# RWKV-7 chunk products written in turn to both column halves, on one Trainium2 core

## The chip, the cores and the metric

The kernel is one program on one core of a Trainium2 chip. The metric is the device time of one launch in microseconds (us), lower is better. The core has engines that run side by side, each in the order in which its instructions were written down: PE (TensorE, matrix products out of SBUF into PSUM; its weight loads are listed as PEld), DVE (VectorE) and ACT (ScalarE), which can both read PSUM, POOL (GpSimd), and SP (SyncE), which issues most DMAs. An engine waits where its next instruction needs something that another has not done yet, and everything behind that instruction waits with it.

## The reference

One layer of a hybrid block over T = 2064 tokens (16 learned ones and 2048 of input) with width 1024: a combined input projection, three head groups beside each other (an RG-LRU recurrence, attention with a forgetting gate, RWKV-7), an output projection with a norm, and a gated feed-forward part with a short convolution. The change touches only the RWKV-7 group, which has 4 heads of 64. For each head it runs this recurrence over a 64x64 state S:

```python
def step(S, inp):
    r_t, w_t, k_t, v_t, kk_t, a_t = inp
    s_kk = jnp.einsum('bhij,bhj->bhi', S, kk_t)
    S = S * w_t[:, :, None, :] - s_kk[..., None] * (kk_t * a_t)[:, :, None, :] + v_t[..., None] * k_t[:, :, None, :]
    return S, jnp.einsum('bhij,bhj->bhi', S, r_t)
_, o = lax.scan(step, s0, xs)
mean = jnp.mean(o, axis=-1, keepdims=True)
var = jnp.mean(jnp.square(o - mean), axis=-1, keepdims=True)
o = ((o - mean) * lax.rsqrt(var + GN_EPS)).reshape(bsz, t, RWKV_WIDTH) * ln_w + ln_b
```

## The kernel before, in words

**Stages.** The input projection runs in three parts over tokens (tiles psp; lines L168 to L170 are the three products of a split fp32 product). Beside it a second stream of work is threaded in, `recurrences`: the gates, the RG-LRU blocks and the RWKV blocks. Attention follows (scores sc at L659 and L660, maxima mx at L530, values po at L682), then the output projection, the feed-forward part up and down. The RWKV work is longer than the projection: its blocks 5 to 8 run beside attention.

**An RWKV block** (`Rwkv.block`, `Rwkv.chunks`) is 4 chunks of 64 tokens, the ninth and last block one chunk. An item is a chunk of one head; a block has ni = 16 items (m2 = 8 chunk pairs of two heads: p is the pair of heads, h the head in it). `sc` holds an item's score matrices, `w3` its transposed operands. The recurrence within a chunk becomes a triangular solve (16x16 blocks on POOL and DVE, joined into 32 and then 64 wide by the small products L1158 into `xf`). The products behind the solve are the ones that change:

- L1198: 16 products a block, 64 rows by 64 columns with 64 moving columns, eight in one PSUM tile, all into partitions 0 to 63. ACT copies each tile into `w3` (L1201).
- L1207: 16 products with 128 moving columns, four in a tile, partitions 0 to 63. DVE copies the left half of each into `ap` (tile xu, L1208), ACT the right half into `w3` (L1209).
- L1222: 16 products like L1207's in size, but head h writes to partitions 64h to 64h+63, so that neighbours take turns. DVE adds the tile to `gt` and `rp` (L1223 and the next line).
- L1234 and L1242, the states: one PSUM tile `gain` holds the gain of all four chunks (L1234, 128 rows), and then chunk after chunk the old state is multiplied in (L1242, four products a chunk) and DVE copies the new state out to `st` (L1246), which the next chunk needs.
- L1274 and L1279, the outputs: for head 0 and then for head 1 a PSUM tile is filled by `rp` times state (L1274) and by scores times values (L1279); the chunks take turns between the two partition halves. Then come the mean and variance over a head on DVE.

**PSUM.** All of these tiles (`self.ps()`, rps in the profile) come from one tag with two buffers: a third tile waits until the first has been copied out.

**What sets the order.** The program's text gives each engine's instructions and their dependencies, and the framework's scheduler, which runs over a simulated timeline, sets the order in which they stand on each engine, RWKV's products among those of the projection and of attention. So an edit of one product moves others too. In the rows of the order below, the names are tiles with buffer numbers (out<-operands), and x8 means eight products in a row.

Of the kernel before, what the change touches and what calls it, by code (L numbers as in the profile page):

```python
# [12 lines left out]
AF = mybir.ActivationFunctionType  # L13
# [5 lines left out]
P = 128  # L19
# [924 lines left out]
class Rwkv:  # L944
# [127 lines left out]
    def chunks(self, b, nch, sg, rav, bk, wc, bon):  # L1072
# [120 lines left out]
        yield  # L1193
        for i0 in range(0, ni, 8):
            m = min(8, ni - i0)
            ps = self.ps().rearrange("p (i t) -> p i t", t=64)
            for i in range(m):
                nc.tensor.matmul(  # L1198
                    ps[0:64, i], sc[64:128, i0 + i, 128:192], w3[64:128, i0 + i, 0:64], start=True, stop=True
                )  # L1200
            nc.scalar.activation(w3[0:64, i0 : i0 + m, 64:128], ps[0:64, :m], AF.Copy)  # L1201
        ap = self.t([P, 2, ni, 64], "xu")[0:64, 0]
        for i0 in range(0, ni, 4):
            m = min(4, ni - i0)
            ps = self.ps().rearrange("p (i t) -> p i t", t=P)
            for i in range(m):
                nc.tensor.matmul(ps[0:64, i], xf[:, i0 + i], w3[0:64, i0 + i], start=True, stop=True)  # L1207
            nc.vector.tensor_copy(ap[:, i0 : i0 + m], ps[0:64, :m, 0:64])  # L1208
            nc.scalar.activation(w3[0:64, i0 : i0 + m, 0:64], ps[0:64, :m, 64:128], AF.Copy)  # L1209
        yield  # L1210
# [19 lines left out]
        for c in range(nch):  # L1230
            for h in range(2):
                for p in range(2):
                    j = 2 * (p * nch + c) + h
                    nc.tensor.matmul(  # L1234
                        gain[64 * h : 64 * h + 64, c, p], sc[:, j, 0:64], w3[:, j, 0:64],
                        start=c == 0 and p == 0, stop=False, skip_group_check=True,
                    )
        for c in range(nch):
            for h in range(2):
                hs = slice(64 * h, 64 * h + 64)  # L1240
                for p in range(2):
                    nc.tensor.matmul(  # L1242
                        gain[hs, c, p], gt[hs, p * nch + c], st[hs, c, p], start=False, stop=True,
                        skip_group_check=True,
                    )
            nc.vector.tensor_copy(st[:, c + 1], gain[:, c])  # L1246
# [14 lines left out]
        v4 = lambda t: t.rearrange("p q a h t -> p (q a) h t")  # L1261
        for h in range(2):
            hs = slice(64 * h, 64 * h + 64)
            ps = self.ps()[:, : P * ntl].rearrange("p (q a t) -> p q a t", a=2, t=64)

            for kind in range(2):
                for p in range(2):
                    for c in range(nch):
                        q, u = divmod(c, 2)
                        pc = p * nch + c  # L1270
                        j = 2 * pc + h
                        dst = ps[64 * u : 64 * u + 64, q, p]
                        if kind == 0:
                            nc.tensor.matmul(  # L1274
                                dst, rp[hs, pc], st[hs, c, p], start=p == 0 and q == 0, stop=False,
                                skip_group_check=True,
                            )
                        else:
                            nc.tensor.matmul(  # L1279
                                dst, sc[:, j, 64:128], w3[:, j, 0:64], start=False, stop=True, skip_group_check=True  # L1280
                            )
            mh = mean[:, :, h : h + 1]
# [877 lines left out]
```

## Time and profile before

| what | us |
|---|---|
| median of 3 runs | 3096.74 |
| lowest and highest of them | 3089.53, 3121.2 |
| the profiled execution | 3106.4 |
| its span | 3104.7 |
| PE busy in the 335 us from 865 | 296.53 |
| PE busy with RWKV's products before 865 and after | 139.64, 110.44 |
| busy in L1198, L1207 | 21.41, 37.78 |
| busy in L1222, L1234 | 18.57, 10.30 |
| busy in L1242, L1274, L1279 | 17.72, 19.60, 12.72 |

The profile is of one execution. An engine's busy time is the time in which at least one of its instructions ran; matmuls overlap, so a line's mean times its count is more than its busy time. In the timeline rows a stretch is a run of like instructions on one engine. The granted clock is the share of TensorE's full clock that the throttle let through.

### The profile page before, as it was taken

Reading aid. Unit: us, or ns where it says so; the run is one execution under the profiler, and the core shown is the slowest. Engines: PE = TensorE matmul, PEld = TensorE weight load, DVE = VectorE, ACT = ScalarE, POOL = GpSimd, SP = SyncE. Lnnn points to the kernel's source line nnn. Section 1 sums busy time; section 2 is a strip of 40 time slices with the busy share of each in tenths; the row PEclk is TensorE's granted clock in tenths of the full one; section 3 lists DMA queues with packets and bytes.
Section 4 is the critical chain, followed back from the end, with each engine's and each line's share of the span. In section 5 each row is a group of like instructions: output and inputs, shape, how many; then the busy total and the mean of one; then the engine's idle time right before and its main releaser. Section 6 shows DMA issues by size and latency. Waiting matters only on the chain.

```text
span 3104.7 us, 52180 instructions
## 1 busy us (share of the span) xinstructions
PE 2923.7 (94%) x18488; PEld 2496.3 (80%) x18488; DVE 2167.8 (70%) x4231; ACT 1462.1 (47%) x2770; POOL 1302.0 (42%) x1436
## 2 busy tenths in 40 slices
PE   6998999999979998899989899999999999999998
PEld 6987988998856664565558899999999999787776
DVE  6247655676688678677635889897778777547766
ACT  4145434344534444445544555566666665324333
POOL 3310101100124465445743568743533334556765
PEclk8999999999968789999999999999999999999999
DMA  6664333353353235543336555565665565535444
GB/s 210 223 203 141 105 96 100 106 142 106 94 128 90 67 84 132 127 114 102 87 99 200 158 181 168 169 197 168 164 168 162 168 187 160 180 101 173 149 161 143
DMA packets 455478, 443.71 MB, mean 143 GB/s; under 512 B 81472, under 2 KB 372490, under 8 KB 452384
## 3 DMA queue, kind: packets, MB, share of 16 engines
q1 hardware_dynamic: 454832, 439.98, 48.3%
q8 instruction: 145, 2.38, 0.3%
q14 instruction: 117, 0.96, 0.1%
q0 software_dynamic: 384, 0.39, 0.0%
HBM read 314.39 MB, written 125.87 MB: 142 GB/s over the span
## 4 chain that ended last, share of the span: by engine, by line
PE 63%; DVE 12%; DMA 11%; POOL 6%; issue 4%; ACT 3%; SPq 1%; POOLq 0%; DVEq 0%; ACTq 0%
PE psu L168 7%; PE psu L169 7%; PE psu L170 7%; PE psp L169 4%; PE psp L170 4%; PE psp L168 4%; PE po L682 3%; PE psd L169 2%; PE psd L168 2%; PE psd L170 2%; PE pswo L168 2%; PE pswo L170 2%; PE pswo L169 2%; DVE uw L1569 2%; PE mx L530 2%
## 5 line engine op out<-in xcount | busy, mean ns | idle before, releaser
L168 PE MATMUL psu<-xo,uw 128*128 128x344 f32 x1848 | 592.7, 325 | 23.3 <-DVE vb L1724 11.7
L169 PE MATMUL psu<-xo,uw 128*128 128x344 f32 x1848 | 594.2, 322 | 0.0
L170 PE MATMUL psu<-xo,uw 128*128 128x344 f32 x1848 | 583.9, 321 | 0.0
L170 PE MATMUL psp<-xh,wl 128*128 128x384 f32 (+2 forms) x1152 | 378.3, 329 | 3.2 <-DVE wl L163 3.2
L168 PE MATMUL psp<-xh,wh 128*128 128x384 f32 (+2 forms) x1152 | 380.5, 330 | 0.0
L169 PE MATMUL psp<-xl,wh 128*128 128x384 f32 (+2 forms) x1152 | 378.3, 328 | 0.0
L168 PEld LDWEIGHTS psu<-xo,uw 128*128 128x128 f32 x1848 | 348.2, 189 | 30.3 <-DVE vb L1724 15.1
L1569 DVE TENSOR_TENSOR uw<-uq,uw 128x512 fp32r<-128x512 f32 x352 | 333.9, 955 | 53.2 <-ACT uw L1568 49.6
L169 PEld LDWEIGHTS psu<-xo,uw 128*128 128x128 f32 x1848 | 349.5, 189 | 0.3 <-DVE xo L1569 0.3
L170 PEld LDWEIGHTS psu<-xo,uw 128*128 128x128 f32 x1848 | 347.8, 189 | 0.0
L1568 ACT ACTIVATE uw<-uq 128x512 fp32r<-128x512 f32 x462 | 286.4, 627 | 89.0 <-PE psu L170 38.4
L664 ACT ACTIVATE p<-sc,bias 128x512 f32<-128x512 f32 (+4 forms) x352 | 197.2, 591 | 189.8 <-PE sc L660 165.1
L1680 DVE SCALAR_TENSOR_TENSOR uy<-psu,ffn_cols,uy 128x342 f32<-128x342 f32 (+1 forms) x396 | 223.6, 566 | 70.6 <-ACT uy L1678 69.6
L703 POOL TENSOR_TENSOR acc<-acc,p 128x512 f32<-128x512 f32 (+3 forms) x208 | 227.3, 1095 | 82.5 <-DVE acc L703 41.8
L1686 POOL TENSOR_TENSOR uy<-uy,uy 128x342 f32<-128x342 f32 (+1 forms) x132 | 147.7, 1119 | 226.8 <-DVE uy L1680 92.9
L170 PEld LDWEIGHTS psp<-xh,wl 128*128 128x128 f32 x1152 | 219.3, 190 | 10.0 <-issue 4.8
L169 PEld LDWEIGHTS psp<-xl,wh 128*128 128x128 f32 x1152 | 219.1, 190 | 7.2 <-issue 5.1
L168 PEld LDWEIGHTS psp<-xh,wh 128*128 128x128 f32 x1152 | 219.1, 190 | 6.5 <-issue 3.8
L533 DVE TENSOR_REDUCE mc<-mx 128x1 f32<-128x400 f32 (+6 forms) x320 | 172.3, 555 | 70.0 <-PE mx L530 66.7
L1569 POOL TENSOR_TENSOR uw<-uq,uw 128x512 fp32r<-128x512 f32 x110 | 158.2, 1438 | 136.5 <-ACT uw L1568 116.1
L1569 DVE TENSOR_TENSOR fo<-u,fo 128x896 fp32r<-128x896 f32 x88 | 105.3, 1198 | 123.1 <-ACT fo L1568 123.1
L1641 POOL TENSOR_TENSOR uq<-uq,uq 128x512 f32<-128x512 f32 x88 | 129.5, 1473 | 117.0 <-DMA uq<-in_ffn_up_dram 82.6
(460 smaller groups left out, 6483.8 us busy)
## 6 DMA issues: line engine op xcount, KB each, us to landing
uq<-in_ffn_up_dram SPq DMA_DIRECT2D x220, 256.0 KB
uq<-scr_us SPq DMA_DIRECT2D x176, 256.0 KB
raw<-in_w_in_dram SPq DMA_DIRECT2D x72, 512.0 KB
scr_us<-uq SPq DMA_DIRECT2D x88, 256.0 KB
u<-scr_ff SPq DMA_DIRECT2D x88, 256.0 KB
scr_ff<-uy SPq DMA_DIRECT2D x110, 171.0 KB
q<-scr_qh SPq DMA_DIRECT2D x96, 128.0 KB
ds<-in_ffn_down_dram SPq DMA_DIRECT2D x10, 1024.0 KB
```

What stands on the lines that cost most here:

```text
L168: nc.tensor.matmul(out, ah, bh, start=first, stop=False, skip_group_check=more)
L169: nc.tensor.matmul(out, ah, bl, start=False, stop=False, skip_group_check=more)
L170: nc.tensor.matmul(out, al, bh, start=False, stop=last, skip_group_check=more)
L533: self.reduced = nc.vector.tensor_reduce(mc[:rows, i, ci : ci + 1], ps[:rows, :full], axis=AX.X, op=ALU.max)
L664: last = nc.scalar.activation(p[:rows, :w], ps[:rows, :w], AF.Exp, bias=bias[:rows, j : j + 1])
L682: mm = nc.tensor.matmul(po[at : at + 64, c0:n], v1[:rows, j], p[:rows, : n - c0], start=start and i < 2, stop=end and i + 2 >= len(group), ...
L703: eng.tensor_tensor(a, ps_[0][0][:rows, c0:n] if start and i == 1 else a, p[:rows, : n - c0], op=ALU.add)
L1568: core.nc.scalar.activation(hi, src, AF.Copy)
L1569: (eng or core.nc.vector).tensor_tensor(lo, src, hi, op=ALU.subtract)
L1641: core.nc.gpsimd.tensor_tensor(raw[:], self.raw[x][:], self.raw[y][:], op=op)
L1680: stt(y[:, :n], src[:, i : n + i], cw[:, 44 * i + cc : 44 * i + cc + 1], y[:, :n], op0=ALU.mult, op1=ALU.add)
L1686: core.pooled = nc.gpsimd.tensor_tensor(v[:, :n], g[:, :n], v[:, :n], op=ALU.mult)
```

## The change

The first and second products behind the solve go to both column halves of the array: one PSUM tile takes twice as many items, the first half of them into partitions 0 to 63 and the second half into 64 to 127, and neighbouring products take turns. So there is one tile of 16 items where there were two of 8, and two of 8 where there were four of 4; each tile is copied out by twice as many copies of the old size, half of which now read partitions 64 to 127. In the states the loops over p and h change places, so that heads alternate product by product. In the outputs both heads' tiles are taken at once and the products with the state alternate between heads.

```diff
-        for i0 in range(0, ni, 8):
-            m = min(8, ni - i0)
+        side = lambda u: slice(64 * u, 64 * u + 64)
+        for i0 in range(0, ni, 16):
+            m = min(16, ni - i0) // 2
             ps = self.ps().rearrange("p (i t) -> p i t", t=64)
             for i in range(m):
-                nc.tensor.matmul(
-                    ps[0:64, i], sc[64:128, i0 + i, 128:192], w3[64:128, i0 + i, 0:64], start=True, stop=True
-                )
-            nc.scalar.activation(w3[0:64, i0 : i0 + m, 64:128], ps[0:64, :m], AF.Copy)
+                for u in range(2):
+                    j = i0 + m * u + i
+                    nc.tensor.matmul(ps[side(u), i], sc[64:128, j, 128:192], w3[64:128, j, 0:64], start=True, stop=True)
+            for u in range(2):
+                j = i0 + m * u
+                nc.scalar.activation(w3[0:64, j : j + m, 64:128], ps[side(u), :m], AF.Copy)
...
-        for i0 in range(0, ni, 4):
-            m = min(4, ni - i0)
+        for i0 in range(0, ni, 8):
+            m = min(8, ni - i0) // 2
             ps = self.ps().rearrange("p (i t) -> p i t", t=P)
             for i in range(m):
-                nc.tensor.matmul(ps[0:64, i], xf[:, i0 + i], w3[0:64, i0 + i], start=True, stop=True)
-            nc.vector.tensor_copy(ap[:, i0 : i0 + m], ps[0:64, :m, 0:64])
-            nc.scalar.activation(w3[0:64, i0 : i0 + m, 0:64], ps[0:64, :m, 64:128], AF.Copy)
+                for u in range(2):
+                    j = i0 + m * u + i
+                    nc.tensor.matmul(ps[side(u), i], xf[:, j], w3[0:64, j], start=True, stop=True)
+            for u in range(2):
+                j = i0 + m * u
+                nc.vector.tensor_copy(ap[:, j : j + m], ps[side(u), :m, 0:64])
+                nc.scalar.activation(w3[0:64, j : j + m, 0:64], ps[side(u), :m, 64:128], AF.Copy)
...
         for c in range(nch):
-            for h in range(2):
-                for p in range(2):
+            for p in range(2):
+                for h in range(2):
                     j = 2 * (p * nch + c) + h
                     nc.tensor.matmul(
                         gain[64 * h : 64 * h + 64, c, p], sc[:, j, 0:64], w3[:, j, 0:64],
...
         for c in range(nch):
-            for h in range(2):
-                hs = slice(64 * h, 64 * h + 64)
-                for p in range(2):
+            for p in range(2):
+                for h in range(2):
+                    hs = slice(64 * h, 64 * h + 64)
                     nc.tensor.matmul(
                         gain[hs, c, p], gt[hs, p * nch + c], st[hs, c, p], start=False, stop=True,
...
-        for h in range(2):
-            hs = slice(64 * h, 64 * h + 64)
-            ps = self.ps()[:, : P * ntl].rearrange("p (q a t) -> p q a t", a=2, t=64)
...
+        both = [self.ps()[:, : P * ntl].rearrange("p (q a t) -> p q a t", a=2, t=64) for _ in range(2)]
+        for p in range(2):
+            for c in range(nch):
+                q, u = divmod(c, 2)
+                pc = p * nch + c
+                for h in range(2):
+                    hs = slice(64 * h, 64 * h + 64)
+                    nc.tensor.matmul(
+                        both[h][64 * u : 64 * u + 64, q, p], rp[hs, pc], st[hs, c, p], start=p == 0 and q == 0,
+                        stop=False, skip_group_check=True,
+                    )
+        for h, ps in enumerate(both):
+            for p in range(2):
+                for c in range(nch):
+                    q, u = divmod(c, 2)
+                    j = 2 * (p * nch + c) + h
+                    nc.tensor.matmul(
+                        ps[64 * u : 64 * u + 64, q, p], sc[:, j, 64:128], w3[:, j, 0:64], start=False, stop=True,
+                        skip_group_check=True,
+                    )
```

The lines have new numbers afterwards: L1198 becomes L1201 (its copy L1204), L1207 becomes L1212 (its copies L1215 on DVE and L1216 on ACT), L1222 becomes L1229, L1234 becomes L1241, L1242 becomes L1249, L1274 becomes L1276, and L1279 becomes L1285.

What becomes of the order is shown at three places, all on PE. The first is block 0, beside the projection; before, around the first products' second tile (rps_2828) and the second products' first tiles:

```order
L168 MATMUL psp_3897<-xh_2867,wh_3891 128x384
L1198 MATMUL rps_2828<-rww_237_1835,rwsc_1834 64x64 x8
L1207 MATMUL rps_2839<-rww_237_1835,rwxf_2631 64x128 x4
L1020 MATMUL eps_3513<-rwwa_3484,wa_up 128x256
L169 MATMUL psp_3897<-xl_2868,wh_3891 128x384
```

The same place afterwards, where the first products stand together some 22 projection products earlier:

```order
L170 MATMUL psp_3894<-xh_2864,wl_3889 128x384
L1212 MATMUL rps_2838<-rww_237_1835,rwxf_2631 64x128 x8
L1212 MATMUL rps_2851<-rww_237_1835,rwxf_2631 64x128 x8
L1020 MATMUL eps_3510<-rwwa_3481,wa_up 128x256
L168 MATMUL psp_3922<-xh_2866,wh_3888 128x384
```

The first products have become one group of 16, and the second two groups of 8 with nothing between them, where there were four groups of 4 at three places.

The second place is block 5, beside attention; before, the last second products and L1222:

```order
L1207 MATMUL rps_9346<-rww_1028_7505,rwxf_9037 64x128 x4
L659 MATMUL sc_11130<-q_1517_10931,k_1471_10803 128x400
L1222 MATMUL rps_9355<-rwsc_7504,rwxu_9324 64x128 x8
L530 MATMUL mx_11068<-k_1472_10804,q_1474_10808 128x400
L660 MATMUL sc_11130<-q_1470_10801,k_1472_10804 128x400
L659 MATMUL sc_11161<-q_1517_10931,k_1471_10803 128x272
L660 MATMUL sc_11161<-q_1470_10801,k_1472_10804 128x272
L530 MATMUL mx_11071<-k_1472_10804,q_1474_10808 128x512
L1222 MATMUL rps_9366<-rwsc_7504,rwxu_9324 64x128 x8
```

Afterwards, from the second products to the second group of L1229:

```order
L1212 MATMUL rps_9309<-rww_1016_7493,rwxf_9022 64x128 x8
L1212 MATMUL rps_9322<-rww_1016_7493,rwxf_9022 64x128 x8
L1020 MATMUL eps_9619<-rwwa_9593,wa_up 128x256
L545 MATMUL mx_10888<-ident,sh_10886 4x128
L530 MATMUL mx_10917<-k_1448_10783,q_1445_10776 128x144
L1229 MATMUL rps_9337<-rwsc_7492,rwxu_9308 64x128 x8
L530 MATMUL mx_10922<-k_1448_10783,q_1445_10776 128x272
L660 MATMUL sc_10966<-q_1456_10802,k_1448_10783 128x512
L660 MATMUL sc_10971<-q_1456_10802,k_1448_10783 128x512
L1020 MATMUL eps_9622<-rwwa_9593,wa_up 128x256
L530 MATMUL mx_10927<-k_1448_10783,q_1445_10776 128x400
L1229 MATMUL rps_9348<-rwsc_7492,rwxu_9308 64x128 x8
```

The groups are fewer and longer, and three rows stand between the second products and the group that reads what is copied out of them.

The third place is the end of block 0, the last step of the states and the outputs (of the projection products ahead of the second head, one is shown); before:

```order
L1242 MATMUL rps_3121<-rwst_3119,rwgt_3095 64x64 x4
L1274 MATMUL rps_3229<-rwst_3119,rwrav_1741 64x64 x5
L1279 MATMUL rps_3229<-rww_237_1835,rwsc_1834 64x64 x8
L168 MATMUL psp_4390<-xh_2867,wh_4384 128x384
L1274 MATMUL rps_3249<-rwst_3119,rwrav_1741 64x64 x8
L1279 MATMUL rps_3249<-rww_237_1835,rwsc_1834 64x64 x8
```

And afterwards:

```order
L1249 MATMUL rps_3118<-rwst_3116,rwgt_3092 64x64 x4
L1276 MATMUL rps_3226<-rwst_3116,rwrav_1741 64x64 x5
L1285 MATMUL rps_3226<-rww_237_1835,rwsc_1834 64x64 x8
L1047 MATMUL eps_3613<-rwix_3520,spr 128x256
L168 MATMUL psp_4224<-xh_2866,wh_4190 128x384
L1276 MATMUL rps_3227<-rwst_3116,rwrav_1741 64x64 x8
L1285 MATMUL rps_3227<-rww_237_1835,rwsc_1834 64x64 x8
```

The two heads' tiles of the outputs (rps_3229 and rps_3249 before, rps_3226 and rps_3227 afterwards) are filled one after the other in both.

More of the change, by code (lines that the diff above doesn't have):

```diff
@@ L1261, in chunks @@
         v4 = lambda t: t.rearrange("p q a h t -> p (q a) h t")
-        for h in range(2):
-            hs = slice(64 * h, 64 * h + 64)
-            ps = self.ps()[:, : P * ntl].rearrange("p (q a t) -> p q a t", a=2, t=64)
[L1266 to L1281, printed above, removed]
+        both = [self.ps()[:, : P * ntl].rearrange("p (q a t) -> p q a t", a=2, t=64) for _ in range(2)]
[18 more added lines that the diff above has]
+                    )
             mh = mean[:, :, h : h + 1]
```

## The prediction, made before the run

> **What bounds the kernel now.** I read the busy table and the chain of waits first, then busy time by stage, then PE's waits, and last the timeline of PE at the products that change.
>
> ```profile
> span 3104.7 us, 52180 instructions
> PE 2923.7 (94%) x18488; PEld 2496.3 (80%) x18488; DVE 2167.8 (70%) x4231; ACT 1462.1 (47%) x2770; POOL 1302.0 (42%) x1436
> PE 63%; DVE 12%; DMA 11%; POOL 6%; issue 4%; ACT 3%; SPq 1%; POOLq 0%; DVEq 0%; ACTq 0%
> ```
>
> PE is busy 94% of the span and carries 63% of the chain; no other engine is near. By stage (columns: length, then busy us and count of PE, PEld, DVE, ACT, POOL, then granted clock, DMA share, GB/s):
>
> ```profile
> 0.00:865.00 865.00, 813.01 (x6541) 747.33 (x6541) 524.59 (x1233) 354.88 (x634) 128.62 (x183) 0.97 0.46 138
> 865.00:1200.00 335.00, 296.53 (x2371) 198.35 (x2373) 253.04 (x772) 141.72 (x301) 147.21 (x239) 0.79 0.39 93
> ```
>
> The first row is the input projection, with RWKV blocks 0 to 4 beside it; the second is the start of attention, with blocks 5 to 8 beside it. All products that change lie in these two. PE's waits there (us in total, times, longest):
>
> ```profile
> PE eps L1014 <- ACT rwe L1015: 11.2, 1, 11.2
> PE psp L170 <- DVE wl L163: 3.2, 1, 3.2
> PE sc L659 <- ACT p L664: 10.0, 29, 1.5
> ```
>
> In the projection PE waits a handful of times (the 11.2 us ahead of the first product that changes), so there time taken off PE comes off the end. In the second stage PE is busy 296.53 / 335 = 0.885, so I let that share of a saving through.
>
> **The products now.** Timeline of PE: start, length of the stretch, line, tiles, shape, passes. Each fp32 product is two passes (132 products, 264 passes a line).
>
> ```profile
> 385.90 1.14 PE L1198 MATMUL rps<-rww,rwsc 64*64 64x64 f32 x16
> 391.74 0.22 PE L1198 MATMUL rps<-rww,rwsc 64*64 64x64 f32 x1
> 396.23 1.96 PE L1207 MATMUL rps<-rww,rwxf 64*64 64x128 f32 x16
> 409.42 1.09 PE L1222 MATMUL rps<-rwsc,rwxu 64*64 64x128 f32 x16
> 410.44 1.20 PE L1234 MATMUL rps<-rww,rwsc 128*64 128x64 f32 x32
> 423.43 0.46 PE L1242 MATMUL rps<-rwst,rwgt 64*64 64x64 f32 x8
> ```
>
> L1222 already writes its products in turn to partitions 0-63 and 64-127, which L1207 does not; with the same weights, width and count it takes 1.09 us where L1207 takes 1.96. L1234 also uses both halves and passes 32 times in 1.20 us.
>
> **Edit 1, second products (L1207, now L1212).** From 1.96 to 1.09 us per 16 passes: 0.87 / 16 x 264 = 14.4 us. The price could be missed only if the new line did not overlap as L1222 does; both read one row half and write two column halves, so I take L1222's.
>
> **Edit 2, first products (L1198, now L1201).** Alone, 16 passes take 1.14 us and another 16 would take 1.14 - 0.22 (the tail of one pass) = 0.92, so 32 cost 2.06; L1234's 32 passes of the same width cost 1.20. 0.86 / 32 x 264 = 7.1 us. Bounds: 0, should 64-wide passes from one row half not overlap, and 7.1; L1234 has the same 32 passes in a row and the same halves, so 7.1. The Trainium skill's page "TensorE: Matmul & The Clock Gate" (section "Wait — 56ns, not 53.3ns?") says that with hardware decode off the sequencer spends about 62 ns on every matmul, which binds once the array work is shorter. By that rule edit 2 would save nothing; L1234's 1.20 us for 32 passes speaks against it.
>
> Per stage (the counts of passes are in these rows, L1198's pair first, then L1207's):
>
> ```profile
> 0.00:865.00 865.00, 11.41 (x160) 10.04 (x160) 0.97 0.46 138
> 865.00:1200.00 335.00, 9.99 (x104) 8.88 (x104) 0.79 0.39 93
> ...
> 0.00:865.00 865.00, 21.26 (x160) 16.91 (x160) 0.97 0.46 138
> 865.00:1200.00 335.00, 16.52 (x104) 13.15 (x104) 0.79 0.39 93
> ```
>
> Of 14.4 + 7.1 = 21.5 us at full clock, 160/264 = 13.0 lie in the projection and 8.5 in attention.
>
> **Edit 3, states (L1234 and L1242, heads innermost).** L1234 is at (1.20 - 0.22) / 31 = 0.032 us a pass, and L1242's 8 passes take 0.46 with a tail of 0.22, so 0.034 for each further one: both halves run already. Nothing to win but one pass of 0.06 at the end of a stretch: 0 us. **Edit 4, outputs.** The order shows L1274 and L1276 in the same groups: head 0's first, then L1279's eight, then head 1's. The second tile is the buffer that the state product holds until its last copy. 0 us.
>
> **Fewer changes of the array's form.** L1201 stands in 9 pieces where L1198 stood in 17, L1212 in 9 where L1207 stood in 30. Counted over PE's whole order, adjacent rows differ in form (full, 64x64, 32x32, 128x64 and so on) 447 times before and 379 after; 50 of the 68 lost ones stand ahead of the last projection product, 18 behind it. The price of one, from a two-pass piece between projection products:
>
> ```profile
> 413.67 0.34 PE L168 MATMUL psp<-xh,wh 128*128 128x384 f32 x1
> 413.93 0.32 PE L1274 MATMUL rps<-rwst,rwrav 64*64 64x64 f32 x2
> 414.19 0.44 PE L169 MATMUL psp<-xl,wh 128*128 128x384 f32 x1
> 414.47 0.33 PE L170 MATMUL psp<-xh,wl 128*128 128x384 f32 x1
> 414.64 0.34 PE L168 MATMUL psp<-xh,wh 128*128 128x384 f32 x1
> ```
>
> From 413.67 to 414.47 are 0.80 us for two projection products, which otherwise start 0.17 apart: 0.46 over, of which two passes are 0.12. So 0.34 for in and out, 0.17 for one change: 8.5 us in the projection, 3.1 in attention. Bounds: 0 (if the joined pieces only wait where they were split) and that.
>
> **What moves with it.** Copies out of PSUM stay as they were in size and nearly in number (one more each on L1201's, L1208's and L1209's successors); half now read partitions 64-127 and write 0-63:
>
> ```profile
> L721 ACT ACTIVATE oh<-po 64x512 f32<-64x512 f32 x24 | 14.3, 595 | 24.7 <-PE po L682 22.5 <-PE mx L733 2.1
> L1201 ACT ACTIVATE rww<-rps 64x512 f32<-64x512 f32 x16 | 9.4, 588 | 9.0 <-PE rps L1198 9.0
> L1208 DVE COPY rwxu<-rps 64x256 f32<-64x256 f32 x33 | 13.6, 412 | 24.4 <-PE rps L1207 24.4
> L1209 ACT ACTIVATE rww<-rps 64x256 f32<-64x256 f32 x33 | 12.2, 369 | 14.7 <-DVE rwxu L1208 14.6
> ```
>
> L721 already copies across the halves at 595 ns against 588, so no price. But a bank is now emptied by two copies of 0.59 (L1204), or by two of 0.41 and two of 0.37 in turn: 1.56 us instead of 0.78, and the next group waits for it. In block 0 some 22 projection products of 0.17 = 3.7 us stand between and cover it. In attention the cover is thin: behind the second L1212 stand L1020, L545 and one small L530 before L1229. There PE, and all attention queued behind L1229, may wait. I take 2 us for the stage, between 0 and 13 (below, the evacuation rival). SP and POOL hold as many rows as before; in attention a few loads of q and k shift by some places among themselves. The nearest wait is ACT's exponentials (10.0 us in all): 0, inside the bounds.
>
> **The sum.** Projection: (13.0 + 8.5) / 0.97 = 22.1. Attention: (8.5 + 3.1) / 0.79 x 0.885 = 13.0. Less 2: 33.1 us. The profiled execution took 3106.4 us (span 3104.7), so 3073.3; it was 9.7 above the median of 3096.74, so 3064 as a median. Behind 1200 us no product changes: 0.
>
> **Rivals.** *Evacuation:* the waits for the copies eat attention's whole gain. For it: the thin cover, and 14.6 us in which L1209 waits for L1208. Against: blocks 5 to 8 only, 1 to 3 us each. 3064 + 13 = 3077. The Trainium skill's page "TensorEngine Tiling (Array Packing)", Performance Considerations, warns of this under "PSUM Bottleneck": tiling speeds up TensorE but not the emptying of PSUM.
>
> *The clock falls (slower than before).* Where small products are many, the granted clock is low (all of PE, then the RWKV products alone):
>
> ```profile
> 1000.00:1040.00 40.00, 38.58 (x345) 26.99 (x346) 20.77 (x72) 18.82 (x45) 16.36 (x29) 0.56 0.27 64
> 1040.00:1080.00 40.00, 35.75 (x284) 22.61 (x281) 31.39 (x98) 16.61 (x36) 20.18 (x33) 0.89 0.34 82
> ...
> 1000.00:1040.00 40.00, 18.48 (x285) 16.41 (x284) 4.63 (x8) 4.03 (x8) 0.56 0.27 64
> 1040.00:1080.00 40.00, 12.16 (x178) 9.40 (x179) 5.20 (x15) 1.51 (x3) 0.89 0.34 82
> ```
>
> If new gaps and closer packed small products bring the stage from 0.79 to c, PE's 296.5 us grow by 296.5 x (0.79/c - 1): the gain is gone at 0.71 (33 us); at 0.70 the time is 3064 + 38 = 3102, and past 1% slower (3128) from 0.65. Against: less RWKV time on PE is less of what goes with the low clock. The Trainium skill's page "TensorE: Matmul & The Clock Gate" (Part 1) has idle time of PE bring the clock down and activity release it. Here it was at 0.56 with PE busy 38.58 of 40, so by that rule alone the way it goes is not told.
>
> *The clock rises:* at 0.84 in the stage, 296.5 x (1 - 0.79/0.84) = 18 less: 3046.
>
> *64-wide pairs do not overlap:* edit 2 is lost, 4.3 / 0.97 + 2.8 / 0.79 x 0.885 = 8 us: 3072.
>
> **How the numbers follow.** The forecast 0.60 (3052 to 3076), evacuation 0.17, clock up 0.13, clock down 0.07, no overlap 0.03. Three runs of the kernel before lie between 3089.53 and 3121.2, so 1% (31 us) is about what a measurement can tell from no change; faster by that is below 3066, in the middle of my forecast. Faster: 0.35 of the forecast and the clock's 0.13, 0.48. Slower, above 3128: 0.04. The rest, 0.48, within 1%. The range reaches from the clock's rise with a little more (3040) to the evacuation's 3077 with half of the changes of form (6) and some clock (5), 3088; it leaves out the clock's fall and the tails.
>
> **What would show it.** L1212 should take some 18.6 us of busy time in all and L1201 about 10.3, as L1222 (first two rows) and L1234 have for the same passes:
>
> ```profile
> 0.00:865.00 865.00, 11.06 (x160) 8.64 (x160) 0.97 0.46 138
> 865.00:1200.00 335.00, 7.51 (x104) 5.82 (x104) 0.79 0.39 93
> ...
> 0.00:865.00 865.00, 6.00 (x160) 5.31 (x160) 0.97 0.46 138
> 865.00:1200.00 335.00, 4.30 (x104) 3.70 (x104) 0.79 0.39 93
> ```
>
> The last projection product should come some 22 us earlier, and L1276 be unchanged. Waits of L1229 on L1215 or L1216 above 3 us would speak for evacuation; a granted clock off 0.79 by 0.05 or more in attention's first 335 us, for the clock. The forecast is wrong if the projection's end does not move.

## The result, and the profile after

The changed kernel takes 3062.6 us (median of 6 runs, 3055.54 to 3070.97) where the kernel before takes 3100.4 beside it (6 runs): ratio 0.988, with a 95% interval of 0.9856 to 0.9905. In a second session with the same kernel it took 3062.92 us, ratio 0.9899 (0.9882 to 0.9915). The forecast of 3064 us holds for the total. Its parts do not all hold, and the experiments below are about that.

First the head of the page of the changed kernel: span, busy time of each engine, and the chain that ended last.

```profile
span 3063.9 us, 52156 instructions
PE 2878.3 (94%) x18488; PEld 2465.2 (80%) x18488; DVE 2169.9 (71%) x4232; ACT 1465.5 (48%) x2772; POOL 1309.6 (43%) x1436
PE 62%; DVE 12%; DMA 11%; POOL 7%; issue 4%; ACT 3%; SPq 1%; POOLq 0%; DVEq 0%; ACTq 0%
```

PE still bounds the kernel, with 45 us less busy time in as many products; the other engines are as busy as before. To see where the span became shorter, I cut both traces at the last product of the projection and at the last product of attention's maxima (mx), which stands near attention's end. The columns are those of the prediction's stage rows. The kernel before:

```profile
0.00:863.00 863.00, 812.07 (x6538) 746.92 (x6539) 522.62 (x1230) 354.50 (x633) 127.00 (x182) 0.97 0.46 138
863.00:1596.70 733.70, 660.49 (x3951) 413.65 (x3949) 530.20 (x1408) 338.07 (x648) 391.40 (x502) 0.89 0.40 100
1596.70:3104.70 1508.00, 1451.16 (x8001) 1335.72 (x8001) 1115.01 (x1594) 769.54 (x1489) 783.62 (x752) 0.98 0.55 167
```

And the changed kernel:

```profile
0.00:844.90 844.90, 792.89 (x6538) 735.77 (x6539) 524.21 (x1239) 355.66 (x633) 124.85 (x182) 0.97 0.47 141
844.90:1548.70 703.80, 635.41 (x3952) 395.51 (x3951) 531.20 (x1400) 339.75 (x650) 398.09 (x502) 0.92 0.41 103
1548.70:3063.90 1515.20, 1449.99 (x8001) 1333.91 (x8001) 1114.47 (x1594) 770.12 (x1489) 786.65 (x752) 0.99 0.54 166
```

The projection is 18.1 us shorter (forecast 22.1), attention 29.9 (forecast 13 less 2), and the rest 7.2 longer (forecast 0) at nearly the same PE busy time. No product is changed in that last stage; in the other profiles of this study it lies between 1506.8 and 1513.4 us, so the changed kernel's is the longest of all, by 1.8 us, and why its pauses grew by 8.4 us stays open. In attention, PE's busy time fell by 25.1 us and its pauses (length less busy time) from 73.2 to 68.4.

One more measure is used below, "RWKV's products at full clock": every product into an rps tile is counted from its start to the start of the next one on PE, without pauses, and time at half clock counts half. In the projection they took 126.9 us before and 106.3 after, so 20.6 less (forecast 13.0 + 8.5), in attention 77.2 and 70.2, so 7.0 less (forecast 8.5 + 3.1).

The changed products themselves, in the timeline of PE at block 0 (start, length, line, tiles, shape, passes):

```profile
383.66 1.15 PE L1201 MATMUL rps<-rww,rwsc 64*64 64x64 f32 x32
...
390.96 1.96 PE L1212 MATMUL rps<-rww,rwxf 64*64 64x128 f32 x32
```

Both lines now run 32 passes in the time that 16 took before (1.14 and 1.96 us). Their busy time over the two stages, first L1201 and then L1212:

```profile
0.00:845.00 845.00, 5.74 (x160) 0.97 0.47 141
845.00:1180.00 335.00, 4.72 (x104) 0.85 0.44 107
...
0.00:845.00 845.00, 10.11 (x160) 0.97 0.47 141
845.00:1180.00 335.00, 9.97 (x104) 0.85 0.44 107
```

In all that is 10.5 us for L1201 (forecast 10.3) and 20.1 for L1212 (18.6). The granted clock in attention's first 335 us went from 0.79 to 0.85. PE's longest waits in attention (us in total, times, longest):

```profile
PE mx L530 <- DMA k<-scr_cl: 13.5, 6, 3.5
PE sc L659 <- ACT p L664: 9.8, 29, 1.3
PE mx L545 <- DVE sh L543: 6.1, 2, 5.7
PE rps L1091 <- DVE rww L1318: 4.3, 1, 4.3
PE sc L659 <- DMA q<-scr_qh: 4.2, 1, 4.2
...
PE rps L1229 <- ACT rww L1216: 0.9, 1, 0.9
```

L1229 waits once for a copy out of PSUM, 0.9 us. The prediction had taken 2 us, and had named 3 as the sign of the evacuation rival.

### The profile page after: what moved, and what is told of

The parts are those of the page before. It is cut to its first block, busy times and chain, and to the rows that moved or that the text cites. A ratio compares the mean times of both kernels' runs of the same rounds, so it can differ in the third digit from the quotient of the medians.

```text
span 3063.9 us, 52156 instructions
## 1 busy us (share of the span) xinstructions
PE 2878.3 (94%) x18488; PEld 2465.2 (80%) x18488; DVE 2169.9 (71%) x4232; ACT 1465.5 (48%) x2772; POOL 1309.6 (43%) x1436
## 4 chain that ended last, share of the span: by engine, by line
PE 62%; DVE 12%; DMA 11%; POOL 7%; issue 4%; ACT 3%; SPq 1%; POOLq 0%; DVEq 0%; ACTq 0%
PE psu L168 7%; PE psu L169 7%; PE psu L170 7%; PE psp L169 4%; PE psp L170 4%; PE psp L168 4%; PE po L682 3%; PE mx L530 2%; DMA u<-scr_ff 2%; PE pswo L168 2%; PE pswo L170 2%; PE pswo L169 2%; PE sc L659 2%; PE psd L168 2%; PE psd L169 2%
```

## The experiments

Each kernel is timed against the kernel before on the same chip. Stage lengths are those of one profile each, cut at the same two products; "half clock" is the time in attention for which the trace's clock records show 0.5. The kernel before was at 3096.83 us beside e1 to e4, at 3095.18 beside after2, e5, e6 and e8, at 3097.61 beside e9 to e12. A stage length can stand high or low with its profiled execution: e6's took 3078.58 us, 9 below its median, e3's 6 above.

| run | what | median us (runs) | ratio, 95% interval | projection | attention | half clock | pauses of PE in attention |
|---|---|---|---|---|---|---|---|
| before | | 3100.4 (6) | 1 | 863.0 | 733.7 | 155 | 73.2 |
| after | all edits | 3062.6 (6) | 0.988 [0.9856, 0.9905] | 844.9 | 703.8 | 118 | 68.4 |
| after2 | the same again | 3062.92 (6) | 0.9899 [0.9882, 0.9915] | 844.4 | 700.7 | 115 | 67.7 |
| e1_second | edit 1 alone | 3088.19 (12) | 0.9975 [0.9957, 0.9993] | 849.4 | 729.7 | 149 | 81.0 |
| e2_first | edit 2 alone | 3088.57 (12) | 0.9968 [0.9947, 0.9988] | 854.0 | 727.0 | 143 | 72.7 |
| e3_heads | edits 3 and 4 alone | 3097.75 (12) | 1.0001 [0.998, 1.0022] | 859.8 | 733.9 | 157 | 66.7 |
| e4_halves_in_line | one half's products after the other's | 3062.34 (6) | 0.9895 [0.9863, 0.9926] | 847.5 | 701.5 | 107 | 67.6 |
| e5_small_pairs | after, 32-wide products paired too | 3082.08 (12) | 0.9963 [0.9948, 0.9978] | 833.3 | 736.9 | 166 | 85.6 |
| e6_no_heads | edits 1 and 2 | 3087.79 (12) | 0.9975 [0.9958, 0.9992] | 839.6 | 724.0 | 129 | 83.1 |
| e8_same_half | after, all in one half | 3089.34 (12) | 0.9989 [0.9975, 1.0004] | 862.5 | 715.6 | 136 | 65.0 |
| e9_fill | after, with wide filler products | 3175.92 (4) | 1.0252 [1.0227, 1.0277] | 841.9 | 820.1 | 269 | 112 |
| e10_copies_turned | after, two copies exchanged | 3083.89 (9) | 0.9958 [0.9942, 0.9973] | 843.1 | 729.9 | 143 | 81.1 |
| e11_no_heads_turned | e6, four copies exchanged | 3073.97 (6) | 0.9925 [0.9906, 0.9945] | 841.5 | 715.2 | 133 | 70.9 |
| e12_small_turned | e5, two copies exchanged | 3052.6 (5) | 0.9863 [0.984, 0.9886] | 830.2 | 720.7 | 147 | 77.0 |

The changed kernel once more (after2) shows how well one kernel's stages repeat: attention differs by 3.1 us and half clock by 3, so the low half-clock time wasn't the luck of one execution.

### One edit at a time: e1_second, e2_first, e3_heads, e6_no_heads

These are the kernel before with a part of the diff shown above: L1207's products as the change has them (e1), L1198's (e2), the loops of states and outputs (e3), and both product edits without those loops (e6).

e1_second:

> Edit 1 alone: only the 16 products with 128 moving columns go to both column halves. By the terms of the prediction: 9.0 us of overlap in the projection, 6.4 in attention, and 22 fewer changes of the array's form (11 ahead of the last projection product, 11 behind) at 0.17, 3.7: 19 us, so about 3081 against 3100. Theory of the clock (attention's 30 us came mostly from a higher granted clock, which rises whenever small products take less time on PE): attention gains more than 10 us by itself and its time at half clock falls from about 143 us to about 120. Theory of the order (attention's gain came from rows that happened to be placed better): attention's part can go either way, by up to 20 us.

e2_first:

> Edit 2 alone: only the 16 products with 64 moving columns go to both column halves. By the terms: 4.4 us of overlap in the projection, 3.1 in attention, and 53 fewer changes of form (39 ahead of the last projection product, 14 behind), 9 us: 17 us, so about 3083. If changes of form cost nothing by themselves: 3093. If 64-wide passes did not overlap: 3091. Theory of the clock: time at half clock in attention falls as well, from about 143 us to about 130.

e3_heads:

> Edits 3 and 4 alone: heads alternate in states and outputs, the first and second products as before. By the prediction 0 from the products; the order has 10 changes of form more in the projection and 14 fewer in attention, so within 3 us of before, 3097 to 3103, and attention's time at half clock stays near 143 us. Theory of the order: its attention rows are rewritten too, so if placement made attention's gain, this kernel may show 10 us or more either way in attention with nothing of the products saved.

e6_no_heads:

> Edits 1 and 2 without edits 3 and 4 (heads in states and outputs as before). By the prediction the same as the changed kernel within 3 us, 3062; the order has 241 and 151 changes of form against 237 and 142, 2 us more. Edits 1 and 2 alone gave 9 us and 8 us, and the whole 38: if the heads add what is missing, this kernel stands near 3080. If the two edits together lift the granted clock in attention where one does not, it is near 3062 with attention's time at half clock near 100 us in its first part.

Measured: the projection ends 13.6 us earlier with edit 1, 9.0 with edit 2, 23.4 with both, 3.2 with the heads alone. So in the projection the two product edits add up (the whole has 18.1, in yet another order). The times do not: the edits alone give 8.6, 8.3 and nothing, and the two product edits together 7.4 us, not the sum. With the heads' loops, which are worth nothing alone, the whole is worth 31 to 37. Both single edits came out longer than the terms gave (3088 against 3081 and 3083), neither lowered half clock as the theory of the clock wanted (149 and 143 us), and in e3 attention didn't move at all, though its rows were placed anew. The missing part is in attention: 724.0 us in e6, 703.8 in the changed kernel. Its row in e6 and two of its waits:

```profile
839.60:1563.60 724.00, 640.90 (x3952) 395.53 (x3951) 529.61 (x1410) 338.55 (x650) 390.25 (x502) 0.91 0.40 101
```

```profile
PE rps L1212 <- ACT rww L1204: 2.8, 2, 1.7
...
PE rps L1229 <- ACT rww L1216: 2.3, 2, 1.5
```

PE is busy 5.5 us longer there than in the changed kernel and pauses 14.7 us longer. The waits on the copies, which the evacuation rival spoke of, do turn up in this order, but with 5.1 us they are a third of it.

Reading the order of PE's products with and without the heads' loops tells which of them matters (from the programs alone; these two were not run). With edit 4 taken out of the changed kernel, each of PE's 15,997 products stands where it stood. With edit 3 taken out, 2,089 of those places hold another product. Edit 3 exchanges products within a tile of states, and the scheduler's simulated timeline comes out another way.

### Without the overlap: e8_same_half

```diff
-                    nc.tensor.matmul(ps[side(u), i], sc[64:128, j, 128:192], ...
+                    nc.tensor.matmul(ps[0:64, i], sc[64:128, j, 128:192], ...
...
-                    nc.tensor.matmul(ps[side(u), i], xf[:, j], w3[0:64, j], ...
+                    nc.tensor.matmul(ps[0:64, i], xf[:, j], w3[0:64, j], ...
```

The copies read partitions 0 to 63 in the same way. Of each pair of products the first is overwritten, so half of the results of these two lines are lost.

> The changed kernel in which all 16 products of a group write to partitions 0 to 63 of the same tile, the second half of the items over the first half's results (so half of the items' results are lost); same tiles, same number of products and copies, groups of 16 and 8 as in the changed kernel, 247 and 138 changes of form against 237 and 142. No two products can overlap on the column halves. If the overlap carries the gain: the projection ends some 14 us later than in the changed kernel, attention takes 10 us more at equal clock, 3062 + 24 = 3086. If fewer and longer groups carry it: near 3063. Theory of the clock: attention's time at half clock is back near 140 us, and the time is a further 10 us or more above: 3095.

The groups are joined as in the changed kernel, but the column halves aren't used. In the timeline of its block 0, L1201 and L1212 take nearly twice as long:

```profile
385.55 2.07 PE L1201 MATMUL rps<-rww,rwsc 64*64 64x64 f32 x32
...
393.94 3.70 PE L1212 MATMUL rps<-rww,rwxf 64*64 64x128 f32 x32
```

The prediction's estimate for 32 passes of L1198 without overlap was 2.06 us. By stage:

```profile
0.00:862.50 862.50, 806.36 (x6539) 747.45 (x6539) 520.91 (x1232) 354.19 (x633) 124.70 (x182) 0.96 0.46 139
862.50:1578.10 715.60, 650.63 (x3951) 407.55 (x3949) 524.86 (x1407) 337.86 (x650) 392.43 (x502) 0.91 0.41 102
```

Two things follow. In the projection the end moves by 0.5 us: PE is busy 5.7 us less than before and pauses 5.2 us longer. RWKV's products at full clock do take less with the joined groups, 120.2 us instead of 126.9, but that doesn't arrive at the end here; with the overlap they take 106.3, and the end comes 17.6 us earlier. And attention is 18.1 us shorter than before without any product being faster (77.3 us at full clock, before 77.2): 8.2 of it are pauses, and 9.1 are the clock (PE was busy at half clock for 116.2 us instead of 134.5). That cannot be the products. Against the changed kernel attention is 11.8 us longer, near the 10 that were expected, and the whole is 3089 where 3086 was expected from the loss of the overlap.

### The products of one half after those of the other: e4_halves_in_line

```diff
-            for i in range(m):
-                for u in range(2):
+            for u in range(2):
+                for i in range(m):
```

This is done in L1201 and L1212; states and outputs stay as in the changed kernel, with the heads in turn.

> The changed kernel with all products of one column half issued before those of the other: same tiles, same copies, the same 237 changes of form ahead of the last projection product, no two neighbours on different halves. If the overlap of the halves carries the gain, the projection ends some 13 us later than in the changed kernel and attention loses 9 us or more: about 3085. If fewer and longer groups carry it, it stays near 3063. Theory of the clock: the small products' time on PE is back, so attention's time at half clock goes back from about 100 us towards 140.

```profile
384.63 1.90 PE L1201 MATMUL rps<-rww,rwsc 64*64 64x64 f32 x32
...
391.17 2.56 PE L1212 MATMUL rps<-rww,rwxf 64*64 64x128 f32 x32
```

The overlap is smaller, 1.90 us for L1201 where it was 1.15 with turns and 2.07 without any, and 2.56 for L1212 between 1.96 and 3.70. But it isn't gone, although the program issues each half's products in a row. Within one half the passes of L1212 start 109 ns apart, and where the halves take turns in the changed kernel, two start 6 or 7 ns apart. Here such a 6 ns pair stands already behind the fifth pass, where the first half has eight in a row: so products of the second half start before the last ones of the first. The projection ends 2.6 us later than with turns, attention takes 2.3 us less, and the time is the same. As a test of the overlap this run is weak, and nothing came of the 3085 us or of half clock near 140 (it is 107). It does show that attention doesn't follow the products: RWKV's take 74.0 us there at full clock, 3.8 more than in the changed kernel, and the stage is no longer.

### More pairs: e5_small_pairs

```diff
-            for i in range(m):
-                small(ps[:, i], xt[:, i0 + i], u1[:, i0 + i], 0, 0)
-            tt(x1[0:32, g], ps[0:32, :m], xr[0:32, g], op=ALU.add)
+            for i in range(m // 2):
+                for u in range(2):
+                    j = i0 + m // 2 * u + i
+                    small(ps[:, i], xt[:, j], u1[:, j], 32 * u, 0)
+            for u in range(2):
+                hg = slice(i0 + m // 2 * u, i0 + m // 2 * (u + 1))
+                tt(x1[0:32, hg], ps[32 * u : 32 * u + 32, : m // 2], xr[0:32, hg], op=ALU.add)
```

The other two single products of L1158 are paired in the same way.

> The changed kernel in which also the three 32-wide products of one kind behind the solve (one row group, one column group) go to two column groups of 32 in turn, 16 items each, with one more copy each: 3 x 264 passes at 0.032, half of it saved, 12.7 us at full clock; the three more copies a block lie on DVE and ACT. The order has 245 and 149 changes of form against 237 and 142, 2.5 us back. If the overlap carries gains everywhere: 3062 - 10 = 3052. Theory of the clock: attention's time at half clock falls below the changed kernel's and the gain is 15 us or more. Evacuation: the halved stretches wait for two small copies where they waited for one, and it stays at 3062.

The projection ends another 11.6 us earlier, at 833.3. Attention is 33 us longer than in the changed kernel, with more time at half clock than any kernel but e9, and the whole is 20 us slower. Again a gain of products in the one stage, and in the other a loss that no product explains.

### Is it the order? e10_copies_turned, e11_no_heads_turned, e12_small_turned

By now the theory was: beside attention, the place of the rows in PE's queue is worth more than the products, and every edit draws new places. The test leaves all products and copies as they are and exchanges two copies that follow each other. In e10 (on the changed kernel) and e12 (on e5) these are the two of L1204:

```diff
-            for u in range(2):
+            for u in (1, 0):
                 j = i0 + m * u
                 nc.scalar.activation(w3[0:64, j : j + m, 64:128], ps[side(u), :m], AF.Copy)
```

In e11 (on e6) the same is done with the copies behind the second products.

e10_copies_turned:

> The changed kernel with one thing turned: of the two ACT copies behind the first products, that of the second half comes first. Same products, same copies, same sizes. PE's order beside attention is another one after that. Theory of the order: half and more of what attention gained hangs on where the scheduler puts the rows, not on the products, so attention goes from 703.7 to 715 to 735 us and the time to 3075 to 3092; the projection's end stays within 843 to 849. Rival, the gain belongs to the products and the alternation of heads: attention stays at 700 to 707 and the time at 3060 to 3066.

e11_no_heads_turned:

> Edits 1 and 2 without the alternation of heads, with the copies behind the second products turned: the second half's first. Same work as the kernel without the alternation of heads, which had attention at 723.9 us and 3087.8 in all. Theory of the order: attention comes out anywhere from 700 to 735, the time from 3058 to 3098, without a product having changed; with the alternation of heads as the real cause of the 25 us it stays at 718 to 730 and 3082 to 3094.

e12_small_turned:

> The changed kernel with the three 32-wide single products paired on two column groups (as before: projection's end at 833, attention 737, 3082), and with the copies behind the first products turned as in the run beside it, which gives another order beside attention. Theory of the order: the projection's end stays at 830 to 837 and attention can be anything from 700 to 737, so 3045 to 3085; if pairing the small products itself made attention slower, attention stays at 730 to 742 and the time at 3076 to 3090.

All three came out as the theory of the order has it, and outside the ranges of its rivals; e10 is the sharp test, since for e11 and e12 the theory allowed nearly anything. Turning two copies costs the changed kernel 21 us (the intervals 0.9942 to 0.9973 and 0.9882 to 0.9915 lie apart), and it gains e6 14 us and e5 some 30. What the exchange costs by itself is small: the first group of L1212 reads only what the first copy wrote, and now waits for the second, at most 0.59 us in each of attention's four blocks. The waits of e10 have it as 2.1 us:

```profile
PE eps L1047 <- DVE rwix L78: 6.7, 1, 6.7
...
PE eps L1047 <- DVE rwk L1048: 4.6, 1, 4.6
...
PE rps L1212 <- ACT rww L1204: 2.1, 2, 1.8
```

The other two rows are products of RWKV that now stand where DVE isn't ready for them, and everything behind them in PE's queue stands too; in the changed kernel that line waits 0.9 us. An exchange redraws the order on the other engines as well, and whether PE's rows alone make the difference was not separated. The stage as a whole, and its first 40 us:

```profile
843.10:1573.00 729.90, 648.85 (x3952) 398.39 (x3951) 530.76 (x1421) 339.65 (x651) 390.20 (x502) 0.90 0.40 100
...
843.10:883.10 40.00, 19.93 (x80) 13.57 (x78) 37.78 (x109) 8.67 (x18) 10.73 (x15) 0.66 0.79 191
```

The same 40 us in the changed kernel:

```profile
844.90:884.90 40.00, 28.45 (x268) 22.04 (x267) 33.10 (x90) 14.15 (x29) 10.96 (x16) 0.70 0.81 191
```

There attention waits for its loads (DMA is at its busiest, 0.8). In one order 268 passes fill that time, in the other 80. This place alone isn't the measure, though: e3 has 325 passes there and an attention of 733.9 us. Over the stage, e10 is 26.1 us longer than the changed kernel: 13.4 of PE's busy time and 12.7 of pauses. Most of the busy time is the clock's: PE was busy at half clock for 121.9 us instead of 101.1, which is 10.4 us lost; the other 3.0 are there at full clock too, in how closely the products follow each other.

e12 is the lowest time of the study, 3052.6 us. Its interval (0.984 to 0.9886) overlaps both of the changed kernel's, so that it is faster than that one isn't shown; that it is faster than the kernel before is. (Its profiled execution took 3063.53 us, 11 above its median, so its stage lengths stand high.)

### What the clock follows: e9_fill

```diff
+        def filled():
+            ps = self.ps()
+            for _ in range(2 if b >= 5 else 0):
+                nc.tensor.matmul(ps[:, :], k["zero"][:, 0:P], k["zero"][:, :], start=True, stop=True)
+            return ps
...
-            ps = self.ps().rearrange("p (i t) -> p i t", t=32)
+            ps = filled().rearrange("p (i t) -> p i t", t=32)
```

> The changed kernel with two more products of 128 by 128 by 512 zeros ahead of each PSUM tile of the 32-wide products in blocks 5 to 8 (40 in all, each overwritten by the products that follow; nothing of the result changes). At 0.22 us each they cost 8.8 us at full clock. Theory of the columns: the granted clock goes down after 3.41 us in which few columns moved through PE, also where PE had no pause, so the fillers hold it up: half-clock time in attention falls from 118 us to 60 to 90, and attention is 703 + 9 - 14 to 29 = 683 to 703 us, if the order of the rest costs nothing. Rival, the clock follows PE's pauses only: half-clock time stays within 105 to 130, attention 708 to 718, time 3068 to 3078. Should the order of the rest be a worse one, attention can be 20 longer under either; the half-clock time tells them apart even then.

Neither expectation held. The fillers drew an order in which the remaining RWKV work stands in one piece at attention's start, with hardly any of attention's products between. The rows are of all of PE, in stretches of 50 us:

```profile
871.00:921.00 50.00, 39.86 (x389) 28.60 (x388) 36.44 (x100) 17.51 (x37) 6.12 (x11) 0.50 0.10 24
921.00:971.00 50.00, 46.48 (x468) 37.53 (x469) 23.90 (x79) 15.94 (x40) 7.33 (x19) 0.50 0.09 18
971.00:1021.00 50.00, 39.64 (x479) 31.34 (x477) 22.37 (x69) 7.00 (x16) 14.75 (x23) 0.50 0.03 8
1021.00:1071.00 50.00, 28.50 (x217) 19.36 (x213) 25.90 (x99) 4.33 (x11) 1.66 (x2) 0.50 0.25 60
```

The clock is at half for 205 us on end, and PE has to wait inside the blocks as well (16.3 us for one line of DVE), since hardly any other work stands between. So the run doesn't tell what fillers do to the clock in a given order. It does show that an order can cost far more than the edits gain: the time is 113 us longer, of which the 40 fillers take 22 from start to next start. And it has one row that counts: from 921 to 971 us PE is busy 46.48 of 50 us and gets 0.50 all the same. Pauses alone do not decide the clock.

The traces hold a better measure. Their clock records change in steps of 3.41 us. For every such step at full clock I counted the moving columns of the products that start in it (a 64x128 pass counts 128), and PE's pauses in it, over the fourteen profiles of the table; the entry is in how many the next step is at half clock (steps with pauses between 0.3 and 1 us, and those in which the profile's last product has ended, are left out):

```
PE's pauses      under 2400    2400 to 3199   3200 to 3999   4000 columns and more
under 0.3 us     1 of 1        2 of 11        10 of 91       13 of 10183
over 1 us        253 of 267    86 of 120      13 of 93       0 of 94
```

Both tell. At like pauses (1.0 to 1.3 us) the clock fell after 7 of 9 steps under 2400 columns, 13 of 24, 3 of 46 and none of 67 over 4000. At like columns (2400 to 3199) it fell after 2 of 11 steps without a pause and 86 of 120 with a long one. In the lower row the two go together, since a step with long pauses has room for few columns. Without pauses, few columns alone seldom brought the clock down.

The way back shows the columns more clearly. Of the steps at half clock with pauses under 0.3 us, the next was at full clock in 17 of 101 under 2400 columns, 78 of 177, 135 of 177, and 149 of 153 from 4000 on; with pauses over 1 us in none of 276. A step at full clock holds at most some 8000 columns, one at half clock about half of that. A stretch of 64-wide passes that do not overlap (2.07 us for 32) would move 32 x 64 x 3.41 / 2.07 = 3370 columns in a step, the paired ones (1.15 us) 6070, and at half clock half as many, by estimate. So narrow products can keep PE at half clock once it is there, as in e9. The Trainium skill's page "TensorE: Matmul & The Clock Gate" (Part 1) has a free-running window of about 3.4 us after which an idle PE is slowed down and a busy one released; the steps of 3.41 us agree with it. That a PE busy with narrow products may not be released is what these traces add. This is a relation over many steps and not an experiment with one cause changed.

## Why the prediction came out right, and where its parts did not

- **What bounds the kernel.** Right: PE's busy time fell by 45 us, and the span by 41.
- **Edit 1 and edit 2, the products.** Right, with the mechanism shown: the overlap is there at the passes' predicted pace, and without it (e8) the projection ends where it did before. The rival "64-wide pairs do not overlap" is out: 32 passes in 1.15 us are 36 ns each. The Trainium skill's page "TensorE: Matmul & The Clock Gate" ("Wait — 56ns, not 53.3ns?") has about 62 ns for every matmul with hardware decode off; no such floor shows in this trace.
- **Edits 3 and 4.** Zero by themselves is right (e3: 1.0001, 0.998 to 1.0022; L1276 is busy 18.8 us in the changed kernel, before 19.6). What the prediction hadn't seen is that edit 3, worth nothing, decides the order that the whole gets: without edits 3 and 4 (e6) the time is 25 us longer, and 14 of these come back with another order of the same work (e11). Edit 4 moves no product on PE.
- **Fewer changes of form.** The price was about right, but the step that it comes off the end was not shown. It was put at 8.5 us. In e8, with 40 changes fewer in the projection (6.8 us at 0.17), RWKV's products at full clock take 6.7 us less; at the projection's end 0.5 arrived, because PE paused 5.2 us longer and was busy at half clock for 46.2 us instead of 38.0. In e6, with the same joined groups and the overlap, the end moved by 23.4, more than the forecast 22.1. So what joining is worth at the end hangs on the order too, and stays open. In the changed kernel the end moved by 18.1, against 22.1 with the term and 13.4 without it.
- **Attention: the copies' waits.** They are 0.9 us in the changed kernel, where 2 was taken. In another order of the same products they are 5.1 (e6). Both lie between the bounds of 0 and 13, and which it is depends on the order.
- **Attention: the sum.** The step that failed most. It took the saving of the products times PE's busy share, with all else where it was, 13 less 2. Measured were 29.9, and they close like this: all of PE's products at full clock took 584.9 us instead of 593.2, so 8.4, of which RWKV's are 7.0; the pauses fell by 4.8; and PE was busy at half clock for 101.1 us instead of 134.5, worth 16.7. So of the products that change came 7, and most of the rest came of the order and the clock that it gives. The rival "the clock rises" had been given 0.13 and 18 us at 0.84; it was 0.85, and it happened. But it isn't a consequence of the faster products either: e10 has them all, and its attention is 4 us shorter than before.
- **The total.** That it is right to 1.4 us is luck. Attention gave 19 us more than forecast; against that stood 4 us less in the projection, 7 us in the last stage of the profiled run, and 7 because the profiles stand differently to their medians (before 9.7 us above its own at the time, after 3). With another draw of the order the same products were at 3084 (e10), and without edits 3 and 4 at 3088 (e6), the upper edge of the range. The range was wide enough for a reason that it didn't name.

## What to carry to other kernels

Where a scheduler sets the order, an edit has two effects: what its instructions cost, and a new draw of everyone's place. Before a small gain or loss is put down to the edit, draw again with a change that does next to nothing (two independent copies exchanged) and see how far the time moves; here the draws differed by 14 to 30 us, as much as the gain looked for. Where such draws are cheap, take several and keep the best, and judge the edit itself in the stage in which the work around it is fixed, here the projection, whose end moved by only 1.8 to 3.1 us in the three redraws.

## What the runs showed of the hardware that was not expected

- The granted clock goes with the columns that move through PE in 3.41 us as well as with its pauses: 253 of 267 steps with long pauses and under 2400 columns were followed by half clock, none of 94 with long pauses and over 4000. From half clock, a PE without pauses came back after 149 of 153 steps with 4000 columns or more, and after 17 of 101 with under 2400.
- Products that write the two column halves overlap without taking turns in the program, where one half's last meet the other's first, and the second half's first ones start ahead of the first half's last ones: 2.56 us instead of 3.70 for 32 passes, with 1.96 for those that take turns.
